# Bonus sums of an RWKV-7 layer as two accumulating single-pass products of a split operand

## The chip, the cores and the metric

The kernel runs on one core of a Trainium2 chip. A core has TensorE (PE: matmuls, with its weight loads shown as PEld), VectorE (DVE), ScalarE (ACT), GpSimd (POOL) and SyncE (SP, which here only issues DMAs). The engines run beside each other, each taking its own instructions in order, and wait for one another through semaphores. The metric is the device time of one execution in microseconds (us), given as the median of several runs. Times inside the kernel come from one profiled execution, counted from the start of its span.

## The reference

It is one step of a two-layer decoder for a prompt of 272 positions (16 learned meta tokens and 256 others) and 8 samples of one position each: 280 columns in all. Layer A is RWKV-7 time mixing with 64 heads of 64 channels (width 4096), layer B sliding-window attention. What matters here are the last lines of layer A, after the recurrence has given `y`:

```python
y = (y - mean) * lax.rsqrt(var + GN_EPS) * gn_g + gn_b
y = y + jnp.sum(r_h * k_h * r_k, axis=-1, keepdims=True) * v_h
y = y.reshape(B, T, WIDTH).astype(dt) * jax.nn.silu(z)
```

For each position and head, `r * k * r_k` is summed over the head's 64 channels; the sum scales that head's `v`. This term is called the bonus here. All inputs and outputs are float32.

## The kernel before

Activations lie with channels on the 128 partitions and positions along the free dimension, so one tile of 128 rows holds two heads, and the sum over a head's channels runs across partitions.

Weight products are done in three single-pass products each. Both operands are split into a part `hi`, cast to the type float32r on ACT, and a remainder `lo = x - hi`, computed on DVE (`split`, L192: the cast is L195, the subtraction L197). `mm3` (L216) accumulates hi*hi, hi*lo and lo*hi in one PSUM bank (L218, L219, L220). A plain float32 operand goes to TensorE as it is, in one matmul call.

Layer A's weights come in units of 256 input rows by 256 outputs: a DMA into `raw`, the cast `whi`, the subtraction `wlo`, each with five buffers (L199). `products` (L708) walks over them one after another, in pieces of six matmuls: r, k, v and z for each block of channels, and lastly part of the output projection. Layer A proper (`phase_a`, L577) starts after the first blocks of k and v, at about 130 us, and its last pieces run at about 1280 us.

Into this row of weight products, other work is woven by `drive` (L609). It runs generators beside `products`: `preps` (per pair of channel blocks, 16 preparations `prep(u)`, each for four heads), `main` (the chunked recurrence), `decodes` (the samples) and epilogues. Each `yield n` means that the generator goes on n pieces later; `self.pp_free` asks in addition that the single spare PSUM bank was last taken at least three pieces ago. TensorE's instructions keep exactly this written order (`pe_order`). On ACT, DVE, POOL and SP, a planner orders the instructions by a simulated timeline, by readiness and priority; some instructions are told not to go ahead of a given weight subtraction (`issue_after`). Each engine's order is fixed when the kernel is built.

`prep(u)` (L857) does, in this order: load the second matrices of the two low-rank products (`lraw`, L868), split them into `lhi` and `llo` (L871 to L873, one buffer each), four low-rank products `ps_l` by `mm3` (L880), then load k, r, the key norms and v, and form decay, `kk`, `a` and the changed `k` on ACT and DVE; a transpose for the samples (`ps_sm`, L934); and lastly the bonus:

- L944, DVE: `rk = r * r_k * k`, 128x272, once for each of the two channel blocks, into a tile with two buffers (tag "sq", shared with `km`, L900)
- L950, PE: `ps_bo`, the product of `rk` with the constant `crbo`, a 128x128 matrix that holds a 64x64 block of ones for each of the two heads. This sums over each head's channels and puts the sum in all of its 64 rows
- L951, DVE: `v` is multiplied by the sum; L952, ACT: the group norm's bias is added

The first of the two sums is written into PE's order five pieces after `rk` (three in the first two preparations), the second four pieces later. The next odd-numbered preparation begins right behind, with its load; its split is written three pieces later and its first low-rank product four pieces after that. An even-numbered preparation also waits for the step `prep_e` of the one before.

`crbo` is loaded once in phase 0 (L274, L275), by a DMA on SP's queue.

Of the kernel before, what the change touches and what calls it, by code (L numbers as in the profile page):

```python
# [12 lines left out]
F32 = mybir.dt.float32  # L13
F32R = mybir.dt.float32r
# [11 lines left out]
L = NM + SEQ  # L26
# [7 lines left out]
LR = 96  # L34
# [14 lines left out]
C_BO, C_SEL = 368, 496  # L49
# [60 lines left out]
class Kernel:  # L110
# [155 lines left out]
    def params(self):  # L266
        nc, I = self.nc, self.I
        dma = nc.sync.dma_start
        dma(self.ct, I['consts'][:, :C_TOTA])
        dma(self.par, I['consts'][:, C_PAR:])  # L270
        yield

        self.cr = {}
        self.cr[C_BO] = self.cp.tile([128, 128], F32, name="crbo")  # L274
        dma(self.cr[C_BO], I['consts'][:, C_BO:C_BO + 128])  # L275

        self.sel = self.cp.tile([128, 32], F32, name="selt")
        nc.gpsimd.memset(self.sel, 0.0)
        dma(self.sel[:, 0:2], I['consts'][:, C_SEL:C_SEL + 2])
        self.half = self.cp.tile([128, 2], F32, name="half")  # L280
        for i in range(2):
            nc.vector.memset(self.half[:, i:i + 1], 0.5 - i)

        self.par2 = self.cp.tile([128, 128], F32, name="par2")
        ts = nc.gpsimd.tensor_scalar
        ts(self.par2[:, 0:64], self.par[:, P_W0:P_W0 + 64], 0.5, None, op0=ALU.mult)
        ts(self.par2[:, 64:96], self.par[:, P_KA:P_KA + 32], 0.5, None, op0=ALU.mult)
        ts(self.par2[:, 96:128], self.par[:, P_KA:P_KA + 32], -0.5, 1.0, op0=ALU.mult, op1=ALU.add)
# [19 lines left out]
    def phase0(self):  # L308
# [11 lines left out]
        for a, b in ((0, 4), (4, 8), (8, 12), (12, 14), (14, 16)):  # L320
            dma(xz[:, a:b], I['xT'][:, a:b])
        params = self.params()
        next(params)

        sq = dx = ph.tile([128, KT, N], F32, name="dx")
# [531 lines left out]
    def prep(self, u):  # L857
        nc, rp, I = self.nc, self.rp, self.I
# [3 lines left out]
        dma = nc.sync.dma_start  # L862
# [5 lines left out]
        dma(raw, I['lw2'][u])  # L868
        if u:
            yield 3  # L870
        hi = rp.tile([LR, 512], F32R, tag="lhi", name=f"lhi_{u}")  # L871
        lo = rp.tile([LR, 512], F32R, tag="llo", name=f"llo_{u}")
        self.split(hi, lo, raw)  # L873
        ws = [(hi[:, 256 * i:256 * i + 256], lo[:, 256 * i:256 * i + 256]) for i in range(2)]
        wa = [w("cl"), w("ta")]
        for i, (hi, lo) in enumerate(ws):
            for j in range(2):
                yield 3 if i or j else 4 if u else 14, self.pp_free
                ps = self.pp_bank(f"ps_l{i}{j}_{u}")
# [53 lines left out]
        ps = self.pp_bank(f"ps_sm{u}")  # L933
# [8 lines left out]
        def rk_of(j):  # L942
            rk = rp.tile([128, L], F32, tag="sq", bufs=2, name=f"rk{j}_{u}")
            V.scalar_tensor_tensor(rk, rT[:, j, :L], self.pcol(P_RK, p0 + j), kT[:, j, :L], op0=MU, op1=MU)  # L944
            return rk
        rk = [rk_of(j) for j in range(2)]
        for j in range(2):
            yield 5 - j if u > 1 else 3, self.pp_free
            ps = self.pp_bank(f"ps_bo{j}_{u}")
            nc.tensor.matmul(ps[:, :L], self.cr[C_BO], rk[j], start=True, stop=True)  # L950
            tt(vT[:, j, :L], ps[:, :L], vT[:, j, :L], op=MU)  # L951
            A.activation(vT[:, j, :L], vT[:, j, :L], AF.Identity, bias=self.pcol(P_GB, p0 + j))  # L952
        self.U[u] = dict(PC=self.PC, bonus=vT, kT=kT, rT=rT, kk=kk, a=a, cl=cl)
# [1015 lines left out]
```

## Time and profile before

| | |
|---|---|
| time, median of 3 runs | 2121.87 us (2119.55 to 2125.27) |
| profiled execution, time | 2132.89 us |
| its span | 2131.1 us, mean granted TensorE clock 0.989 |
| busy: PE, DVE, ACT | 2073.1 (97%), 1685.4 (79%), 1252.9 us (59%) |
| bonus products `ps_bo` | 64 records on PE, 21.2 us busy, from 176.4 to 1116.8 us |
| bonus scaling L951 on DVE | 32 records, 419 to 442 ns each |
| `rk` L944 on DVE | 32 records, 486 to 502 ns each |

A line of the profile names the source line (L950), the engine, the operation, the tile written and the tiles read (`ps_bo<-rk,crbo`), its shape and how many instructions it groups. "128*128 128x272" on PE means a stationary operand of 128x128 and a moving one of 128x272. In the order of time, a row begins with start and duration in us; where several like instructions follow each other they are merged (x2). A bracket such as [0.93 <-PE ps_r L219] is the idle time of the engine before that instruction, and what ended it. Matmuls overlap in the pipeline, so their durations are longer than the distance from one to the next. One plain float32 matmul call of L950 shows as two records on PE.

### The profile page before, as it was taken

The page shows a single profiled execution, that of the slowest core. Times are in us where ns is not written, and L with a number is a line of the kernel's source. Part 1 is how long each engine was busy: PE and PEld are TensorE (multiplying, and loading weights), DVE is VectorE, ACT ScalarE, POOL GpSimd, SP SyncE. Part 2 cuts the span into 40 slices and gives each one's busy share as a digit, 9 for nine tenths or more (in the row PEclk, how much of TensorE's full clock was granted, in tenths as well). Part 3 has the DMA queues.
Part 4 walks back from the last instruction along what each step waited for, and adds up shares of the span by engine and source line. Part 5 has one row for each costly group of instructions (what it writes and reads, how often), then busy time and mean ns, then how long its engine had stood idle before and what let it go on. Part 6 is the DMA issues. An engine that isn't in the chain of part 4 may idle for free.

```text
span 2131.1 us, 55813 instructions
## 1 busy us (share of the span) xinstructions
PE 2073.1 (97%) x21420; PEld 1971.4 (93%) x21420; DVE 1685.4 (79%) x4080; ACT 1252.9 (59%) x2757; POOL 121.5 (6%) x188
## 2 busy tenths in 40 slices
PE   9999999899999989999999999999999999999997
PEld 7999898899899989999999999999999999999997
DVE  7866767687678768888888787987888888878885
ACT  3456666576765757767675455565565655644443
POOL 0011100001010010100100001100000000000000
PEclk9999999999999999999999999999999999999999
DMA  7997667668657766777656678757455454567774
GB/s 256 315 314 243 177 215 241 183 186 289 208 178 211 251 207 204 214 225 212 203 161 222 217 239 253 237 186 223 143 149 171 137 158 135 178 203 252 227 220 134
DMA packets 276356, 446.28 MB, mean 209 GB/s; under 512 B 54056, under 2 KB 97768, under 8 KB 275696
## 3 DMA queue, kind: packets, MB, share of 16 engines
q1 hardware_dynamic: 275656, 441.66, 66.4%
q8 instruction: 168, 2.75, 0.5%
q10 hardware_dynamic: 432, 1.05, 0.1%
q14 instruction: 100, 0.82, 0.1%
HBM read 381.69 MB, written 65.03 MB: 210 GB/s over the span
## 4 chain that ended last, share of the span: by engine, by line
PE 60%; DVE 3%; DMA 2%; issue 1%; ACT 1%; POOL 0%; POOLq 0%; DVEq 0%; SPq 0%; ACTq 0%
PE ps_z L218 6%; PE ps_z L219 5%; PE ps_z L220 5%; PE ps_ob L218 3%; PE ps_ob L220 3%; PE ps_ob L219 3%; PE ps_q L218 3%; PE ps_q L220 3%; PE ps_q L219 3%; PE ps_oa L219 2%; PE ps_oa L218 2%; PE ps_oa L220 2%; PE ps_o L218 1%; PE ps_o L219 1%; PE ps_o L220 1%
## 5 line engine op out<-in xcount | busy, mean ns | idle before, releaser
L218 PE MATMUL ps_z<-mhlm,whi_z 128*128 128x280 f32 x512 | 158.7, 310 | 0.4 <-ACT st L789 0.4
L220 PE MATMUL ps_z<-mhlm,wlo_z 128*128 128x280 f32 x512 | 149.6, 292 | 2.7 <-issue 2.7
L218 PE MATMUL ps_q<-bmh,whi_qb 128*128 128x264 f32 x512 | 150.0, 293 | 0.4 <-ACT whi_qb L195 0.3
L219 PE MATMUL ps_z<-mhlm,whi_z 128*128 128x280 f32 x512 | 149.8, 292 | 0.0
L218 PE MATMUL ps_z<-bmh,whi_zb 128*128 128x264 f32 x512 | 147.5, 288 | 0.0
L220 PE MATMUL ps_q<-bmh,wlo_qb 128*128 128x264 f32 x512 | 145.6, 284 | 0.6 <-DVE wlo_qb L197 0.6
L219 PE MATMUL ps_q<-bml,whi_qb 128*128 128x264 f32 x512 | 145.6, 284 | 0.0
L219 PE MATMUL ps_z<-bml,whi_zb 128*128 128x264 f32 x512 | 145.4, 284 | 0.0
L220 PE MATMUL ps_z<-bmh,wlo_zb 128*128 128x264 f32 x512 | 145.4, 284 | 0.0
L218 PE MATMUL ps_ob<-ghi,whi_ob 128*128 128x264 f32 x512 | 145.3, 285 | 0.0
L220 PE MATMUL ps_ob<-ghi,wlo_ob 128*128 128x264 f32 x512 | 144.6, 284 | 0.0
L219 PE MATMUL ps_ob<-glo,whi_ob 128*128 128x264 f32 x512 | 144.6, 283 | 0.0
L195 ACT CAST whi_ob<-raw_ob 128x512 fp32r<-128x512 f32 x128 | 79.1, 620 | 96.9 <-PE ps_ob L219 75.4
L195 ACT CAST whi_oa<-raw_oa 128x512 fp32r<-128x512 f32 x128 | 79.2, 620 | 89.7 <-PE ps_oa L219 27.9
L197 DVE TENSOR_TENSOR wlo_r<-raw_r,whi_r 128x512 fp32r<-128x512 f32 x128 | 87.5, 688 | 48.7 <-ACT whi_r L195 46.3
L218 PE MATMUL ps_v<-mhlm,whi_v 128*128 128x280 f32 x384 | 121.4, 316 | 0.4 <-ACT st L789 0.4
L218 PE MATMUL ps_k<-mhlm,whi_k 128*128 128x280 f32 x384 | 120.4, 313 | 1.1 <-ACT st L789 1.1
L197 DVE TENSOR_TENSOR wlo_v<-raw_v,whi_v 128x512 fp32r<-128x512 f32 x128 | 87.4, 687 | 41.0 <-ACT whi_v L195 37.8
L195 ACT CAST whi_v<-raw_v 128x512 fp32r<-128x512 f32 x128 | 79.1, 618 | 66.5 <-PE ps_v L219 39.5
L195 ACT CAST whi_zb<-raw_zb 128x512 fp32r<-128x512 f32 x128 | 78.2, 619 | 62.6 <-PE ps_z L219 39.3
L220 PE MATMUL ps_k<-mhlm,wlo_k 128*128 128x280 f32 x384 | 112.9, 294 | 1.2 <-issue 1.1
L219 PE MATMUL ps_k<-mhlm,whi_k 128*128 128x280 f32 x384 | 113.0, 294 | 0.0
(473 smaller groups left out, 7584.2 us busy)
## 6 DMA issues: line engine op xcount, KB each, us to landing
raw_k<-a_w_rkvz SPq DMA_DIRECT2D x128, 256.0 KB
raw_v<-a_w_rkvz SPq DMA_DIRECT2D x128, 256.0 KB
raw_r<-a_w_rkvz SPq DMA_DIRECT2D x128, 256.0 KB
raw_z<-a_w_rkvz SPq DMA_DIRECT2D x128, 256.0 KB
raw_oa<-a_w_out SPq DMA_DIRECT2D x128, 256.0 KB
raw_qb<-b_w_qz SPq DMA_DIRECT2D x128, 256.0 KB
raw_zb<-b_w_qz SPq DMA_DIRECT2D x128, 256.0 KB
raw_ob<-b_w_o SPq DMA_DIRECT2D x128, 256.0 KB
```

The lines of the kernel that those rows point to most:

```text
L195: self.nc.scalar.copy(hi, src)
L197: return self.nc.vector.tensor_tensor(lo, src, hi.bitcast(F32), op=ALU.subtract)
L218: mm(ps, wh, xh, start=start, stop=False)
L219: mm(ps, wh, xl, start=False, stop=False)
L220: return mm(ps, wl, xh, start=False, stop=stop)
```

## The change

Only layer A's bonus sums change. The block matrix of ones is loaded in phase 0 into a scratch tile and cast on ACT into a float32r tile `ones`. `rk` is split like the weights: a cast on ACT and a subtraction on DVE for each channel block. The sum is then two accumulating single-pass products, hi and lo of `rk`, both with `ones`. Ones are exact in float32r, so no third product is needed.

The two halves of `rk`, for both channel blocks, lie in the buffers of the low-rank matrices (tags "lhi" and "llo"), which are made larger for it: 128x544 where they were 96x512. The places in TensorE's order, the `yield`s, are the same.

```diff
-        self.cr = {}
-        self.cr[C_BO] = self.cp.tile([128, 128], F32, name="crbo")
-        dma(self.cr[C_BO], I['consts'][:, C_BO:C_BO + 128])
+        self.ones = self.cp.tile([128, 128], F32R, name="ones")
+        ones = self.ph.tile([128, 128], F32, name="blocks")
+        dma(ones, I['consts'][:, C_BO:C_BO + 128])
+        nc.scalar.copy(self.ones, ones)
...
-        hi = rp.tile([LR, 512], F32R, tag="lhi", name=f"lhi_{u}")
-        lo = rp.tile([LR, 512], F32R, tag="llo", name=f"llo_{u}")
+        hi = rp.tile([128, 544], F32R, tag="lhi", name=f"lhi_{u}")[:LR, :512]
+        lo = rp.tile([128, 544], F32R, tag="llo", name=f"llo_{u}")[:LR, :512]
         self.split(hi, lo, raw)
...
             rk = rp.tile([128, L], F32, tag="sq", bufs=2, name=f"rk{j}_{u}")
             V.scalar_tensor_tensor(rk, rT[:, j, :L], self.pcol(P_RK, p0 + j), kT[:, j, :L], op0=MU, op1=MU)
-            return rk
-        rk = [rk_of(j) for j in range(2)]
+            self.split(two[0][:, j], two[1][:, j], rk)
+        two = [rp.tile([128, 2, L], F32R, tag=n, name=f"rk{n}{u}") for n in ("lhi", "llo")]
+        for j in range(2):
+            rk_of(j)
         for j in range(2):
             yield 5 - j if u > 1 else 3, self.pp_free
             ps = self.pp_bank(f"ps_bo{j}_{u}")
-            nc.tensor.matmul(ps[:, :L], self.cr[C_BO], rk[j], start=True, stop=True)
+            for i in range(2):
+                nc.tensor.matmul(ps[:, :L], self.ones, two[i][:, j], start=i == 0, stop=i == 1)
             tt(vT[:, j, :L], ps[:, :L], vT[:, j, :L], op=MU)
```

## The prediction

> **What bounds the kernel now.** I read the profile's page first, then the busy times by stage over the part where the changed code runs, then the waits of TensorE there, and last the instructions in order of time around some of the bonus sums.
>
> The page, first line and busy times:
>
> ```profile
> span 2131.1 us, 55813 instructions
> PE 2073.1 (97%) x21420; PEld 1971.4 (93%) x21420; DVE 1685.4 (79%) x4080; ACT 1252.9 (59%) x2757; POOL 121.5 (6%) x188
> ```
>
> The stages of layer A in which bonus sums run (columns: stretch, its length, busy us and instructions of PE, PEld, DVE, ACT, POOL, granted clock, DMA share, GB/s):
>
> ```profile
> 130.00:300.00 170.00, 162.57 (x1704) 156.87 (x1703) 110.91 (x232) 112.31 (x245) 18.62 (x35) 0.97 0.74 227
> 300.00:500.00 200.00, 190.86 (x2348) 177.26 (x2347) 150.42 (x346) 126.96 (x293) 11.62 (x21) 0.98 0.68 212
> 500.00:700.00 200.00, 195.41 (x2614) 182.59 (x2613) 147.14 (x331) 131.99 (x289) 19.57 (x29) 0.98 0.67 207
> 700.00:900.00 200.00, 192.59 (x2333) 178.03 (x2332) 154.13 (x355) 135.07 (x306) 17.46 (x26) 0.98 0.73 228
> 900.00:1100.00 200.00, 193.18 (x2593) 181.84 (x2593) 175.58 (x407) 139.99 (x310) 15.04 (x27) 0.99 0.66 199
> 1100.00:1280.00 180.00, 175.39 (x2176) 165.98 (x2177) 145.52 (x323) 97.72 (x199) 4.61 (x7) 1.00 0.70 221
> ```
>
> PE is busy for 1110.0 of these 1150 us, DVE for 883.7 (77%), with its highest share, 88%, from 900 to 1100. So PE sets the pace, with 40 us of holes, and DVE is the next engine. What PE waits for between 130 and 1280 us, the five longest sums:
>
> ```profile
> PE ps_yt L1271 <- DVE vT L1272: 11.0, 6, 7.3
> PE ps_so L1098 <- DVE TN L1077: 5.5, 2, 4.3
> PE ps_so L1104 <- issue: 3.3, 1, 3.3
> PE ps_sm L934 <- POOL sm L931: 3.2, 1, 3.2
> PE ps_ch L1201 <- ACT W L1192: 2.9, 3, 2.2
> ```
>
> The first two and the last, 19.4 us, are late work of DVE and ACT. The bonus sum itself is not among them. Its matmuls, and one of them in PE's order of time:
>
> ```profile
> L950 PE MATMUL ps_bo<-rk,crbo x64: 390/392/661, 176.4 to 1116.8; 128*128 128x272 f32 x64
> ```
> ```profile
> 409.71 0.29 PE L220 MATMUL ps_v<-mhlm,wlo_v 128*128 128x280 f32 x1
> 409.84 0.62 PE L950 MATMUL ps_bo<-rk,crbo 128*128 128x272 f32 x2
> 410.10 0.49 PE L218 MATMUL ps_v<-mhlm,whi_v 128*128 128x280 f32 x1
> 410.43 0.29 PE L219 MATMUL ps_v<-mhlm,whi_v 128*128 128x280 f32 x1
> ```
>
> The durations overlap, so I count from end to end. L220 ends at 409.71 + 0.29 = 410.00, the pair of records that is one plain float32 product at 410.46, the next L218 at 410.59, L219 at 410.72. The bonus product holds PE for **0.46 us**; a single-pass product of 280 columns for 0.13. Nothing waits around it: before and after it PE runs without a hole.
>
> **The change part by part.**
>
> *PE.* 64 records are 32 products of 0.46 us: 14.7 us go. In their place come 64 single-pass products of 272 columns. That form isn't in the trace; its price is bounded by the 280-column products above (0.13) and the 264-column ones of layer B:
>
> ```profile
> 1459.05 0.28 PE L220 MATMUL ps_q<-bmh,wlo_qb 128*128 128x264 f32 x1
> 1459.18 0.28 PE L218 MATMUL ps_q<-bmh,whi_qb 128*128 128x264 f32 x1
> 1459.30 0.28 PE L219 MATMUL ps_q<-bml,whi_qb 128*128 128x264 f32 x1
> ```
>
> These follow each other in 0.12 to 0.13. I take 0.125, midway: 64 x 0.125 = 8.0 us come. PE saves 14.7 - 8.0 = **6.7 us** (7.0 at 0.12, 6.4 at 0.13). The number of PE records stays 2 per sum, so weight loads and sequencer work don't grow.
>
> The Trainium skill, "TensorE: Matmul & The Clock Gate", section "Back-to-back issue gap", gives N/2.4 + 2.5 ns for a single-pass product, 116 ns for 272 columns; by it, as an estimate, 7.4 us would come and 7.3 go. The trace disagrees by about 10 ns: the rule gives 119 ns for 280 columns, where the rows above show 130.
>
> *ACT and DVE.* The split adds 32 casts on ACT and 32 subtractions on DVE, each of 128x272. Near rows, the first from ACT's order of time, then DVE groups between 160 and 1120 us:
>
> ```profile
> 18.03 0.66 ACT L195 CAST mhld<-mst 128x560 fp32r<-128x560 f32 x1 [3.34 <-DVE mst L390]
> 18.59 1.65 ACT L195 CAST whi_k<-raw_k 128x512 fp32r<-128x512 f32 x3
> ```
> ```profile
> L197 DVE TENSOR_TENSOR wlo_r<-raw_r,whi_r 128x512 fp32r<-128x512 f32 x115 | 78.5, 688 | 37.6 <-ACT whi_r L195 35.3 <-DMA vt<-N 1.2 <-DMA raw_r<-a_w_rkvz 0.8
> ...
> L944 DVE SCALAR_TENSOR_TENSOR rk<-rT,par,kT 128x272 f32<-128x272 f32 x32 | 14.8, 495 | 3.2 <-DMA rT<-rd 3.2
> ```
>
> A cast of 512 elements holds ACT for 1.65/3 = 0.55, so one of 272 for between 0.29 (in proportion) and 0.55; I take 0.35 for the fixed part: 11 us. A subtraction lies between 0.37 (688 x 272/512) and 0.49; at 0.43 it is 14 us. Neither engine is the bound: DVE has 1150 - 883.7 = 266 us idle there, ACT 506. The cover is that idle time. Without it each split costs up to its 0.35 + 0.43 plus two hand-overs, about 1 us. What leaks through: DVE's load rises by 14/884 = 1.6%, and 1.6% of the 19.4 us of waits on DVE and ACT is 0.3; for queueing, which grows faster than load, I take **0.5 us** (0 to 3; a better planned order, which would be a gain, stands with the rivals).
>
> *Latency ahead of the sum.* The product used to need only rk; now it needs rk, a cast on ACT and a subtraction on DVE. The narrowest of the 16 places has rk on DVE at 200.43 and its sum on PE at 206.93:
>
> ```profile
> 200.43 0.50 DVE L944 SCALAR_TENSOR_TENSOR rk<-rT,par,kT 128x272 f32<-128x272 f32 x1
> ```
> ```profile
> 206.93 0.62 PE L950 MATMUL ps_bo<-rk,crbo 128*128 128x272 f32 x2
> ```
>
> That is 6.0 us of slack. The chain needs 0.35 + 0.43 and, in either queue, at worst a pair of 512-element items ahead (1.1 and 1.4): 3.3 us. Cost 0. If the slack were gone, PE would stall in order, with the weight products behind it.
>
> *The shared buffers.* rk's halves take the buffers of the low-rank weights (lhi, llo), one each. So the next preparation's lhi and llo may be written only when the second bonus sum of this one is done. Before, the cast ran long ahead. First pair of preparations, on ACT, DVE and PE:
>
> ```profile
> 162.46 0.62 ACT L195 CAST lhi<-lraw 96x512 fp32r<-96x512 f32 x1
> ...
> 179.32 0.62 ACT L195 CAST whi_r<-raw_r 128x512 fp32r<-128x512 f32 x1 [0.93 <-PE ps_r L219]
> ```
> ```profile
> 176.70 0.68 DVE L197 TENSOR_TENSOR llo<-lraw,lhi 96x512 fp32r<-96x512 f32 x1
> ```
> ```profile
> 179.20 0.62 PE L950 MATMUL ps_bo<-rk,crbo 128*128 128x272 f32 x2
> ...
> 185.05 0.29 PE L218 MATMUL ps_l<-lt4h,lhi 96*128 96x280 f32 x1
> ```
>
> The sum ends at 179.82, the first reader starts 5.2 us later; read the same way, this first pair is the narrowest of the 15. The new chain is a cast (0.62) and a subtraction (0.68) with up to 1.1 and 1.4 queued ahead: 3.8 us. It fits. Queued behind the waiting lhi on ACT are weight casts; but ACT already waits for PE there, as the row at 179.32 shows, so it has time to lose. Cost 0, bounded by 5.2 - 3.8 = 1.4 us of margin.
>
> *Start-up.* The block of ones is loaded into a scratch tile and cast once on ACT, some 0.3 us, at a time when ACT is idle for microseconds at a stretch (3.34 before the row at 18.03); its first reader is at 176.4. Cost 0.
>
> *What stalls swallow.* Saved time is kept only if the next stall's cause moves with PE. The longest stall:
>
> ```profile
> 380.35 0.93 DVE L897 SCALAR_TENSOR_TENSOR kk<-kT,par,kk 128x280 f32<-128x280 f32 x2 [4.76 <-DMA kk<-kr]
> ```
> ```profile
> 386.56 0.90 PE L1271 MATMUL ps_yt<-consts,Y 128*128 128x128 f32 x3 [7.30 <-DVE vT L1272]
> ```
>
> DVE stood there on a DMA of key norms. Eight sums lie before it (4 preparations): 8 x 0.21 = 1.7 us saved. The norms come out of earlier PE products, so part of the stall moves along; I take **0.8 us** lost, half (0 to 1.7).
>
> *Sum.* -6.7 + 0.5 + 0.8 = **-5.4 us**. On the profiled execution's own 2132.9 us (span 2131.1, 1.8 around it) that gives 2127.5. That execution lies 11.0 above the median of the runs; the saving carries over to them: 2121.9 - 5.4 = **2116.5 us**.
>
> **The rivals.** About 0.3% (6.4 us) is what a measurement of this kernel can tell from no change, and the full PE saving is just that size.
>
> *Swallowed.* PE's time goes into the next waits, and the end hardly moves. For it: 19.4 us of PE's waits end on DVE or ACT, which get more work. Against: in the long runs between stalls ACT and DVE wait for PE (the row at 179.32; the 35.3 us of DVE behind ACT's casts follow from the same). If a quarter of 6.7 passes and the 0.5 is added, 2121.9 - 1.7 + 0.5 = 2121.
>
> *The low-rank buffers bind* (the other side). If DVE or ACT brings llo more than 5.2 us after the sum, PE stalls at its first reader. What such a stall costs is to be seen where PE waited 1.23 us:
>
> ```profile
> 672.79 1.20 PE L1125 MATMUL ps_so<-TT,ET 32*32 32x32 f32 x64 [1.23 <-ACT ET L1120]
> ```
> ```profile
> 671.50:674.20 2.70, 1.47 (x67) 1.37 (x67) 2.67 (x6) 1.72 (x3) 0.39 (x1) 1.00 0.89 262
> 674.20:677.70 3.50, 3.50 (x15) 3.27 (x15) 1.51 (x3) 0.99 (x2) 0.28 (x1) 0.51 0.97 263
> ```
>
> After it the granted clock is 0.51 for 3.5 us, which loses 1.7 more: 1.2 + 1.7 = 2.9 us a stall. From three stalls on it eats the saving; at 4 it gives 2121.9 - 5.4 + 11.6 = 2128. The same page of the Trainium skill (section "Why this matters for your kernels") asks only that idle gaps stay under about 3 us; by that a stall of 1.2 us would cost 1.2, four would cost 4.8 and the result be 2121. The trace disagrees: the clock halved after 1.23 us.
>
> *A better order.* ACT and DVE are ordered anew by the planner, and stalls that are accidents of the order can go. One long wait on DVE with its half-clock stretch (4.3 + 1.7 in the second wait above) less gives 2116.5 - 6.0 = 2110.5.
>
> *It doesn't do what it says*: the new products run as slowly as the old one. Then 64 x 0.46 = 29.4 come for 14.7: 2137. Against it: every weight product of this form runs at 0.13.
>
> **How the numbers follow.** Forecast 0.45, own range 2113 to 2120; a third of it lies beyond 0.3%. Swallowed 0.18 (2119 to 2124). Buffers bind, or DVE's load leaks on the same scale, 0.16. Better order 0.20. Not as said 0.01. Faster by over 0.3%: 0.15 of the forecast and 0.19 of the better order, 0.34. Within: 0.30 of the forecast, 0.17 swallowed, 0.01 each of buffers and order, 0.49. Slower: 0.15 of the buffers, 0.01 each of swallowed and not as said, 0.17. The range of 8 in 10 reaches from 2109 (a better order) to 2128 (four stalls).
>
> **What would show it.** Two records of 272 columns per sum, ending 0.12 to 0.13 apart, and PE's time on the sums down from 14.7 to 8.0. lhi's casts right behind the second sum, on ACT, and no wait of ps_l longer than 1 us. The sums no later behind rk than PE's order puts them. Waits of PE on DVE in 130 to 1280 us near 19 us as before. I am wrong if a wait at ps_l or ps_bo shows, if PE's waits on DVE grow by over 3 us, or if the sums take over 0.3 us each.

## The result

| | before | changed |
|---|---|---|
| time, median of 20 runs each | 2124.31 us (2119.55 to 2128.32) | 2118.46 us (2114.5 to 2124.2) |
| ratio to before | | 0.9978, 95% interval 0.9970 to 0.9987 |
| profiled execution, time and span | 2132.89, 2131.1 us | 2118.32, 2116.5 us |
| PE, DVE, ACT busy | 2073.1, 1685.4, 1252.9 us | 2064.9, 1697.8, 1263.8 us |

The change saves 0.22% or, with 2124 us for the whole, 4.7 us (2.8 to 6.4); the two medians themselves differ by 5.9 us. 5.4 us were forecast (2116.5 us, range 2109 to 2128), within the 0.3% called "no change to be told" there. One execution of the products-only kernel below took 5016 us and is in no ratio.

The two profiled executions lie 14.6 us apart, two and a half times the difference of the medians: the one of before is 8.6 us above the median of its 20 runs, the one of the change is at its own. So no sum can be read off the two profiles; single places can. The page of the changed kernel, first line and busy times:

```profile
span 2116.5 us, 55871 instructions
PE 2064.9 (98%) x21420; PEld 1965.8 (93%) x21420; DVE 1697.8 (80%) x4112; ACT 1263.8 (60%) x2790; POOL 122.5 (6%) x188
```

One bonus sum in PE's order of time (start, duration):

```profile
405.52 0.29 PE L220 MATMUL ps_v<-mhlm,wlo_v 128*128 128x280 f32 x1
405.65 0.29 PE L954 MATMUL ps_bo<-rklhi,ones 128*128 128x272 f32 x1
405.78 0.29 PE L954 MATMUL ps_bo<-rkllo,ones 128*128 128x272 f32 x1
405.90 0.29 PE L218 MATMUL ps_v<-mhlm,whi_v 128*128 128x280 f32 x1
```

The ends are 405.81, 405.94, 406.07, 406.19: a product holds PE for 0.13 and 0.13, as the weight products around it do. The split on ACT and DVE (groups between 160 and 1120 us):

```profile
L195 ACT CAST rklhi<-rk 128x272 fp32r<-128x272 f32 x32 | 12.7, 418 | 11.4 <-DVE rk L945 11.4
```
```profile
L197 DVE TENSOR_TENSOR rkllo<-rk,rklhi 128x272 fp32r<-128x272 f32 x32 | 13.1, 434 | 0.5 <-ACT rklhi L195 0.4
```

The shared buffers, at the first pair of preparations, on PE, ACT and DVE:

```profile
177.45 0.29 PE L954 MATMUL ps_bo<-rkllo,ones 128*128 128x272 f32 x1
...
182.97 0.29 PE L218 MATMUL ps_l<-lt4h,lhi 96*128 96x280 f32 x1
```
```profile
178.14 0.62 ACT L195 CAST lhi<-lraw 96x512 fp32r<-96x512 f32 x1
```
```profile
178.88 0.68 DVE L197 TENSOR_TENSOR llo<-lraw,lhi 96x512 fp32r<-96x512 f32 x1
```

lhi, which ran 17 us ahead of the second sum before, now starts 0.4 us behind its end (177.74), and llo is done 3.4 us before the first low-rank product. What PE waits for between 130 and 1280 us (total, times, longest):

```profile
PE ps_yt L1275 <- DVE vT L1276: 8.0, 2, 6.9
PE ps_so L1102 <- DVE TN L1081: 6.1, 2, 3.5
...
PE ps_bo L954 <- ACT vk L854: 2.0, 1, 2.0
...
PE ps_bo L954 <- DVE vT L955: 1.5, 2, 1.3
```

The third row, also a wait for the spare bank (ACT copies a transpose out of it), stood in the kernel before with 1.6 us. The last row is new. No sum waits there for its halves: the second sum of the first preparation waits for DVE to scale the first one and so free the only spare bank.

```profile
177.22 0.39 PE L954 MATMUL ps_bo<-rklhi,ones 128*128 128x272 f32 x1 [1.27 <-DVE vT L955]
```
```profile
170.78 0.46 DVE L197 TENSOR_TENSOR rkllo<-rk,rklhi 128x272 fp32r<-128x272 f32 x1
...
171.76 0.43 DVE L197 TENSOR_TENSOR rkllo<-rk,rklhi 128x272 fp32r<-128x272 f32 x1
...
176.74 0.43 DVE L955 TENSOR_TENSOR vT<-ps_bo,vT 128x272 f32<-128x272 f32 x1
```

Yet the split has a part in it. DVE is busy without a gap from 168.33 to this scaling, and the two subtractions lie in that queue, with 0.38 and 0.36 us to the next start: 0.74 of the 1.27 us. In the second profile of the change (e5 below) this wait doesn't appear.

And the second row shows where the split's work on DVE gets onto the path. DVE's order of time ahead of one of its two waits, PE's wait, and the stage's busy times (columns as in the prediction; the last but two is the granted clock):

```profile
908.28 0.20 DVE L1075 TENSOR_TENSOR stmp<-NL 128x52 f32<-128x52 f32 x1
...
909.09 0.68 DVE L197 TENSOR_TENSOR wlo_z<-raw_z,whi_z 128x512 fp32r<-128x512 f32 x1
909.70 0.43 DVE L197 TENSOR_TENSOR rkllo<-rk,rklhi 128x272 fp32r<-128x272 f32 x1
910.05 0.20 DVE L1077 TENSOR_TENSOR NL<-NL,stmp 128x52 f32<-128x52 f32 x1
910.17 0.43 DVE L197 TENSOR_TENSOR rkllo<-rk,rklhi 128x272 fp32r<-128x272 f32 x1
910.52 0.68 DVE L197 TENSOR_TENSOR wlo_z<-raw_z,whi_z 128x512 fp32r<-128x512 f32 x1
911.12 0.18 DVE L1075 TENSOR_TENSOR stmp<-NL 128x28 f32<-128x28 f32 x1
911.42 0.69 DVE L197 TENSOR_TENSOR wlo_z<-raw_z,whi_z 128x512 fp32r<-128x512 f32 x1
912.03 0.18 DVE L1077 TENSOR_TENSOR NL<-NL,stmp 128x28 f32<-128x28 f32 x1
912.25 1.04 DVE L1081 STREAM_TRANSPOSE TN<-NL 128x512 f32<-128x512 f32 x1
```
```profile
913.43 1.27 PE L1102 MATMUL ps_so<-TN,Noff 32*32 32x16 f32 x81 [2.56 <-DVE TN L1081]
```
```profile
910.80:913.40 2.60, 0.07 (x1) 0.00 (x1) 2.44 (x6) 0.59 (x1) 0.46 (x1) 0.89 1.02 323
913.50:919.60 6.10, 6.10 (x146) 6.03 (x147) 1.26 (x3) 3.96 (x6) 0.20 (x1) 0.50 0.85 278
```

L1075 to L1081 is a chain of small DVE steps (the triangular substitution of the recurrence), and PE needs its end. DVE takes its instructions in order with hardly a gap here, and each of the two subtractions, 0.43 long, stands between two steps of that chain. PE waits 2.56 us and then runs 6.1 us at half clock, which is another 3.05 lost. The same place before, on DVE and PE, with the stage behind it:

```profile
919.47 0.20 DVE L1071 TENSOR_TENSOR stmp<-NL 128x52 f32<-128x52 f32 x1
...
920.88 0.20 DVE L1073 TENSOR_TENSOR NL<-NL,stmp 128x52 f32<-128x52 f32 x1
921.15 0.69 DVE L197 TENSOR_TENSOR wlo_z<-raw_z,whi_z 128x512 fp32r<-128x512 f32 x1
921.76 0.18 DVE L1071 TENSOR_TENSOR stmp<-NL 128x28 f32<-128x28 f32 x1
921.97 0.19 DVE L1073 TENSOR_TENSOR NL<-NL,stmp 128x28 f32<-128x28 f32 x1
922.20 1.03 DVE L1077 STREAM_TRANSPOSE TN<-NL 128x512 f32<-128x512 f32 x1
```
```profile
923.38 1.26 PE L1098 MATMUL ps_so<-TN,Noff 32*32 32x16 f32 x128 [1.24 <-DVE TN L1077]
```
```profile
923.50:929.50 6.00, 6.00 (x283) 5.74 (x279) 3.04 (x7) 4.50 (x7) 0.20 (x1) 1.00 0.86 235
```

There PE waited 1.24 us and the clock stayed whole. From the step at 919.47 to the transpose the chain took 2.73 us; now, from 908.28, it takes 3.97. Of these 1.24 more, the two subtractions make 0.70 (to the next starts); nearly all the rest is a weight subtraction (911.42) that the order before had behind the chain. The longer wait for TN has become shorter (4.3 to 3.5), so that the sum is 6.1 where it was 5.5.

In the runs below, the wait at this place is 1.24 to 1.26 us with no subtraction of rk on DVE (the plain product twice, the products alone in both layouts, one product, the subtraction on GpSimd), 2.56 or 2.57 with one split on DVE (the split alone, the change again, the unread split) and 2.86 with two. Out of line are the buffers alone, 2.34 with no split, and the two kernels with later sums, 4.09 and, without a split, 2.79. The clock behind it varies: in the second profile of the change the half-clock stretch is 3.4 us, half as long as here.

### The profile page after: what moved, and what is told of

It reads as the page before. It is cut to its first block, busy times and chain, and to the rows that moved or that the text cites. A ratio compares the mean times of both kernels' runs of the same rounds, so it can differ in the third digit from the quotient of the medians.

```text
span 2116.5 us, 55871 instructions
## 1 busy us (share of the span) xinstructions
PE 2064.9 (98%) x21420; PEld 1965.8 (93%) x21420; DVE 1697.8 (80%) x4112; ACT 1263.8 (60%) x2790; POOL 122.5 (6%) x188
## 4 chain that ended last, share of the span: by engine, by line
PE 87%; DVE 5%; ACT 3%; DMA 3%; issue 2%; SPq 0%; POOL 0%; DVEq 0%; POOLq 0%; ACTq 0%
PE ps_z L218 6%; PE ps_z L219 6%; PE ps_z L220 6%; PE ps_k L218 3%; PE ps_ob L218 3%; PE ps_ob L220 3%; PE ps_v L218 3%; PE ps_ob L219 3%; PE ps_r L218 3%; PE ps_q L218 3%; PE ps_q L220 3%; PE ps_q L219 3%; PE ps_k L219 3%; PE ps_k L220 3%; PE ps_v L220 3%; PE ps_v L219 3%
## 5 line engine op out<-in xcount | busy, mean ns | idle before, releaser
L218 PE MATMUL ps_v<-mhlm,whi_v 128*128 128x280 f32 x384 | 119.8, 312 | 0.4 <-ACT st L790 0.4
L218 PE MATMUL ps_k<-mhlm,whi_k 128*128 128x280 f32 x384 | 119.1, 310 | 1.0 <-ACT st L790 1.0
L219 PE MATMUL ps_v<-mhlm,whi_v 128*128 128x280 f32 x384 | 112.7, 293 | 0.0
```

What stands on the lines that cost most here:

```text
L218: mm(ps, wh, xh, start=start, stop=False)
L219: mm(ps, wh, xl, start=False, stop=False)
```

## The experiments

Each ratio is to the kernel before, run beside it on the same chip; us are (ratio - 1) x 2124. TensorE's part in the edits: one plain product 0.458 us, one single-pass product 0.125.

**The parts alone.** First the split without the new products. rk is split into the low-rank buffers (enlarged as in the change, not shown below), nobody reads the halves, the plain product stays:

```diff
+            self.split(two[0][:, j], two[1][:, j], rk)
             return rk
+        two = [rp.tile([128, 2, L], F32R, tag=n, name=f"rk{n}{u}") for n in ("lhi", "llo")]
         rk = [rk_of(j) for j in range(2)]
```

> The kernel before, with rk split into hi and lo as in the change (32 casts on ACT, 32 subtractions on DVE, written into the low-rank buffers), but the sum still the plain float32 product of rk; nobody reads the two halves. TensorE's work is that of before. Prediction's theory: the split leaks 0.5 us (0 to 3): ratio to before 1.0002, at most 1.0014. Rival, the engines' load costs as much as half the saving: +3 us or more, ratio 1.0015 or above.

Measured: 1.0003 (0.9994 to 1.0012), +0.6 us (-1.3 to +2.5). As forecast; the rival's +3 lies outside.

The products without the split:

```diff
-            rk = rp.tile([128, L], F32, tag="sq", bufs=2, name=f"rk{j}_{u}")
-            V.scalar_tensor_tensor(rk, rT[:, j, :L], ...)
-            self.split(two[0][:, j], two[1][:, j], rk)
+            V.scalar_tensor_tensor(two[:, j], rT[:, j, :L], ...)
-        two = [rp.tile(...) for n in ("lhi", "llo")]
+        two = rp.tile([128, 2, L], F32R, tag="lhi", name=f"rkhi{u}")
...
-                nc.tensor.matmul(ps[:, :L], self.ones, two[i][:, j], ...)
+                nc.tensor.matmul(ps[:, :L], self.ones, two[:, j], ...)
```

> The changed kernel without the split: DVE writes rk rounded to float32r at once, and both single-pass products read this same tile, so the bonus comes out doubled and rounded. No cast, no subtraction; the tile lies in the buffer of lhi alone. TensorE's work is that of the change. Prediction's theory: -6.7 saved, 0.8 swallowed: -5.9 us, ratio 0.9972. Rival, the split's load leaks 3 us: -8.4 or more here, ratio 0.9960. Rival, stalls swallow the saving: as the change or less, -5 to -2 us.

Measured, over four executions: 0.9954 (0.9941 to 0.9967), -9.8 us (-12.5 to -7.0): more than TensorE's own saving of 6.7. The -5.9 of the prediction's theory lies outside the interval; the number is the one that a leak of 3 us gave. A second layout below tests this.

The shared buffers alone (the low-rank buffers enlarged as in the change, not shown below):

```diff
-            rk = rp.tile([128, L], F32, tag="sq", bufs=2, name=f"rk{j}_{u}")
+            rk = rp.tile([128, 544], F32R, tag=("lhi", "llo")[j], name=f"rk{j}_{u}").bitcast(F32)[:, :L]
```

> The kernel before, with rk of the two channel blocks written into the buffers of lhi and llo (float32 values, as before), so that the next preparation's lhi and llo wait for the bonus sums; no split, the plain float32 product. Prediction's theory: the wait is covered, 0 us, ratio 1.0000 within 0.0007. Rival, the low-rank buffers bind: stalls at the first low-rank product of 1.2 us and more with half clock behind, +3 us each, ratio 1.0015 or above and a wait row for ps_l.

Measured: 0.9996 (0.9987 to 1.0005), -0.8 us (-2.8 to +1.1). The low-rank buffers don't bind. Buffers of their own for rk's halves would take 4.25 kB per partition, and the opposite, the change without sharing, wasn't tried.

The parts don't add up: split and products together would give -9.2 us, and the change gave -4.7. The next runs ask where the rest went.

**How much of TensorE's time reaches the end.** The plain product issued twice:

```diff
-            nc.tensor.matmul(ps[:, :L], self.cr[C_BO], rk[j], start=True, stop=True)
+            for _ in range(2):
+                nc.tensor.matmul(ps[:, :L], self.cr[C_BO], rk[j], start=True, stop=True)
```

> The kernel before with each float32 bonus product issued twice, the second overwriting the first: 32 x 0.46 = 14.7 us more on TensorE, nothing else. Prediction's theory: of the 3.7 us ahead of the long stall half goes into it, the rest passes: +12.9 us, ratio 1.0061. Rival, time on TensorE here goes into or out of the waits: a quarter passes, +3.7 us, ratio 1.0017.

Measured: 1.0047 (1.0033 to 1.0062), +10.0 us (+7.0 to +13.2) for 14.7 us of work. The sums of that run are 128 records on PE, of the same length as before:

```profile
L951 PE MATMUL ps_bo<-rk,crbo x128: 390/392/661, 176.4 to 1119.7; 128*128 128x272 f32 x128
```

0.68 of it passes (0.48 to 0.90). The rival of a quarter is out; the 12.9 of the theory is inside the interval, at its upper side.

**One product instead of two.** The products-only kernel with a single product:

```diff
-            for i in range(2):
-                nc.tensor.matmul(ps[:, :L], self.ones, two[:, j], start=i == 0, stop=i == 1)
+            nc.tensor.matmul(ps[:, :L], self.ones, two[:, j], start=True, stop=True)
```

The change ran once more beside it:

> The changed kernel once more, beside the next three. The split alone cost 0.6 us and the products alone saved 9.8, but the change saved 4.6: either chance (the change comes out at -7 to -9 here, ratio about 0.996), or the split costs some 5 us once the sums read it (ratio 0.9978 again).

Measured for the change again: 0.9984 (0.9970 to 0.9997), -3.4 us (-6.4 to -0.6), in line with the 20 runs.

> rk rounded to float32r by DVE as it writes it, and a single product of it: no cast, no subtraction, the remainder lo left out of the sum. TensorE does 32 x (0.458 - 0.125) = 10.7 us less than before. If 70% of TensorE's time passes on to the end, as in the run with the product twice: -7.3 us, ratio 0.9966. If all of it passes and the split was what held the change back: -10.7 to -14 us, ratio 0.9950 to 0.9934.

Measured: 0.9957 (0.9941 to 0.9972), -9.1 us (-12.5 to -5.9) for 10.7 us less on TensorE: 0.85 passes (0.55 to 1.17), between the two expectations and with both in the interval. Its median is 2113.70 us, that of the change beside it 2121.36. Against the products alone in this layout (-9.8), the 4.0 us that TensorE does less show no gain (+0.7, -3.6 to +5.0 with the intervals combined).

**Does the split cost by its load, or because sums wait for it?** The change with its split, but the products read rk itself:

```diff
-            rk = rp.tile([128, L], F32, tag="sq", ...)
+            rk = rp.tile([128, L], F32R, tag="sq", ...)
-            self.split(two[0][:, j], two[1][:, j], rk)
+            self.split(two[0][:, j], two[1][:, j], rk.bitcast(F32))
+            return rk
...
-                nc.tensor.matmul(ps[:, :L], self.ones, two[i][:, j], ...)
+                nc.tensor.matmul(ps[:, :L], self.ones, rk[j], ...)
```

> The change with its split on ACT and DVE (hi, lo written into the low-rank buffers as in the change), but both single-pass products read rk itself, rounded by DVE as it writes it, so the sums don't wait for the split and the bonus comes out doubled. TensorE's work is that of the change. If the split costs by its load on DVE and ACT: as the change, -4.6 us, ratio 0.9978. If it costs because the sums wait behind cast and subtraction: as the products alone, -9.8 us, ratio 0.9954.

Measured: 0.9997 (0.9981 to 1.0013), -0.6 us (-4.0 to +2.8). The -9.8 of the second expectation is out, and the change itself, where the halves are read, is no slower. By load it should have come out like the change: the -4.6 of the 20 runs lies just outside the interval, the -3.4 of the change beside it inside. What a split costs that nobody reads, the next runs show.

The same kernel without the split, and with two of them (the line of `split` taken out, or written twice; without it the low-rank buffers, too, are those of before):

> The products alone in another layout: both single-pass products read rk as DVE rounds it, in rk's own two buffers as before, and the low-rank buffers are those of before (the bonus comes out doubled). It is the kernel with the unread split, less the split, and less the shared buffers. If the split's load is what costs: -9.8 again, ratio 0.9954, and some 5 us or more under the unread split. If the first such run was helped by its order: -5 to -7, ratio 0.9977 to 0.9967.

> The kernel with the unread split, with cast and subtraction done twice each: 64 casts on ACT and 64 subtractions on DVE for the same products of TensorE (the bonus comes out doubled). If a split costs 5 us by load: another 5 on top of the unread split, ratio about 1.002. By the prediction's 0.5 us a split: as the unread split within 1 us, ratio 0.9995 to 1.0002.

Measured: without 0.9979 (0.9966 to 0.9993), -4.5 us (-7.2 to -1.5); twice 1.0017 (1.0003 to 1.0032), +3.6 us (+0.6 to +6.8). So none, one and two splits give -4.5, -0.6 and +3.6 us, some 4 us each (8.1 for two, 3.9 to 12.3 with the intervals combined). The prediction's 0.5 a split is outside the interval of the last. The two longest waits of PE on DVE in the three kernels, none, one and two splits (130 to 1290 us):

```profile
PE ps_yt L1273 <- DVE vT L1274: 8.5, 4, 6.6
PE ps_so L1100 <- DVE TN L1079: 5.8, 2, 4.6
```
```profile
PE ps_yt L1275 <- DVE vT L1276: 7.3, 3, 6.5
PE ps_so L1102 <- DVE TN L1081: 7.0, 2, 4.5
```
```profile
PE ps_yt L1276 <- DVE vT L1277: 10.3, 4, 8.0
PE ps_so L1103 <- DVE TN L1082: 8.0, 2, 5.1
```

The wait for TN, the end of the chain that the subtractions stood in above, grows from 5.8 to 7.0 and 8.0; both together from 14.3 to 14.3 and 18.3, and all waits of PE on DVE there from 17.1 to 19.4 and 22.2.

The products alone came to -4.5 in this layout and -9.8 in the other, with the same work on every engine. The two differ in the buffers that hold rk and, as each kernel is planned anew, in the order of ACT, DVE and SP; which of them makes the 5 us wasn't shown.

**The subtraction on GpSimd:**

```diff
-            self.split(two[0][:, j], two[1][:, j], rk)
+            A.copy(two[0][:, j], rk)
+            G.tensor_tensor(two[1][:, j], rk, two[0][:, j].bitcast(F32), op=SU)
```

> The change with rk's remainder lo subtracted on GpSimd, which is busy for 6% of the span, in place of DVE: DVE has the 14 us of subtractions less, ACT the same casts. If the split costs by its load on DVE: toward the products alone, -7 to -10 us, ratio 0.9967 to 0.9954. If the load costs little: as the change, -3 to -5 us, ratio 0.9985 to 0.9978. A subtraction on GpSimd should take over 1 us, so sums that come late behind it would show as waits of ps_bo.

Measured: 1.0004 (0.9990 to 1.0017), +0.8 us (-2.1 to +3.6), so the gain of the change is gone. The subtraction there:

```profile
L947 POOL TENSOR_TENSOR rkllo<-rk,rklhi x32: 751/922/1352, 168.0 to 1088.5; 128x272 fp32r<-128x272 f32 x32
```

It takes 0.75 to 1.35 us, and no sum waits for it in the trace. Why freeing DVE of 13 us doesn't show is open: neither "DVE's load alone" nor "the load costs little" gives this number. The trace shows where time came back, not why. Between 130 and 1290 us PE waits 41.1 us in all, where it waited 33.3 in the change, though the wait for TN shown above is back at 1.26. DVE is busy for 902.5 us there, only 8.4 less than in the change, as its weight subtractions take longer (`wlo_r` 710 ns in the mean, 691 in the change).

**Later sums**, and later with one product:

```diff
-            yield 5 - j if u > 1 else 3, self.pp_free
+            yield 7 - j if u > 1 else 5, self.pp_free
```

> The change with the first sum of each preparation written two pieces later into TensorE's order (seven instead of five, five instead of three; the second sum seven minus one, or five): 1.5 us more slack behind the split. If sums wait for the split or for the spare bank: faster than the change by 2 us or more, ratio 0.9968 or below. If the prediction's slack was wide enough: the same as the change, ratio 0.9978 within 0.0008.

> One product of rk as DVE rounds it (lo left out of the sum), with the sums written two pieces later as in the run with later sums. If both gains add: -9.1 - 2 = -11 us, ratio 0.9948. If the later place only moves stalls about: as the one product, ratio 0.9957.

Measured: the change with later sums 0.9972 (0.9957 to 0.9988), -5.9 us (-9.1 to -2.5); one product, later 0.9955 (0.9940 to 0.9970), -9.6 us (-12.7 to -6.4). The first lies between its two expectations and can't be told from the change; the second is the one product's -9.1 again. The later place is worth nothing that these runs show. The one product beats both kernels by some 5 us and more, at the price of rk's remainder.

## Why the prediction was right

The twelve ratios other than that with GpSimd fit, roughly, a sum of two terms: 0.84 of what TensorE's work changes, plus 2.4 us per split (least squares over them, weighted by their intervals). The kernels scatter about it by more than their intervals: some 2 us, and over 4 for the products alone (-4.2) and the doubled split (+4.5). That I put to the planned orders, but it was not shown. By the prediction's steps:

- *PE, -6.7.* Right: the sums' records end 0.125 apart in the median, so 64 x 0.125 = 8.0 us stand where 14.7 did. TensorE's 0.125 is the middle of the bounds that the 264- and 280-column rows gave. The rule of the Trainium skill that the prediction names beside it ("TensorE: Matmul & The Clock Gate", section "Back-to-back issue gap") is given there for an isolated product, which the prediction does not say; by it a sum's product would take 0.116, as an estimate.
- *ACT and DVE, 11 and 14 us.* 12.7 and 13.1 busy. Right.
- *What leaks through, 0.5 (0 to 3).* Probably too small, but inside its own range. The split alone under the old product gives 0.6, the runs with none, one and two splits some 4 us each, the fit 2.4 (1.2 without the doubled split). The step scaled PE's waits by DVE's mean load. But DVE works in order, and some of its chains end in a wait of PE: two subtractions of 0.43 in such a chain delay it by nearly their full length, and PE's stall was followed by half clock. The idle time of DVE elsewhere in the stage doesn't help at that place. This is shown at that place; that it makes the whole of the leak is not. PE's waits on DVE, which were to stay near 19 us, come to 16.7 in the change (19.0 before, and 19.0 in the second profile of the change).
- *What stalls swallow, 0.8 of 6.7.* 0.88 was to pass; the runs give 0.68 and 0.85 for more and less work, the fit 0.84: 1.1 swallowed. Right in size.
- *Latency ahead of the sum, 0.* Right: no sum waits for its halves. The prediction named a wait of ps_bo as a sign against itself, and one of 1.27 us shows, but for the spare bank, which it had not counted. As a sign it was badly chosen: the kernel before has a wait of ps_bo, too, of 1.6 us.
- *The shared buffers, 0.* Right: lhi directly behind the sum, llo 3.4 us ahead of its readers, and 0.9996 for the buffers alone. The rival built on them is out.
- *Start-up, 0.* Right: at 165 us both kernels stand at the same matmul within 0.1 us.

By the two terms the change should have saved 0.84 x 6.7 - 2.4 = 3.2; 4.7 and 3.4 were measured. So the gain of TensorE and the share that passes were right by their mechanism, but that -5.4 came within 1 us of the first number is in part luck: by the fit the leak is 2 us short, and the kernels scatter by as much.

## What to carry to other kernels

Where TensorE is at 97%, count its time from end to end of its products; here some 0.8 of a saving reached the end. Work put onto an engine with a quarter of its time idle need not be free if that engine carries serial chains in order that TensorE waits for: look where the new instructions fall in its queue, not at its mean load. One profiled execution may lie 9 us off the median, so price single places from it and take sums from many runs.

## What was not expected of the hardware

How long a hole of TensorE lowers its clock. The stall before the first bonus sums, in the kernel before and in the changed one, on PE, and the same stretch behind it in each (before first; the granted clock is the last but two):

```profile
172.41 0.42 PE L934 MATMUL ps_sm<-consts,sm 128*96 128x128 f32 x1 [3.17 <-POOL sm L931]
```
```profile
170.37 0.31 PE L935 MATMUL ps_sm<-consts,sm 128*96 128x128 f32 x1 [1.22 <-POOL sm L932]
```
```profile
172.50:175.90 3.40, 3.40 (x16) 3.40 (x16) 2.65 (x7) 1.45 (x3) 0.20 (x1) 0.50 1.01 329
```
```profile
172.50:175.90 3.40, 3.40 (x27) 3.23 (x26) 3.40 (x10) 1.70 (x3) 0.00 (x0) 1.00 0.90 248
```

3.17 us halve the clock for 3.4 us; 1.22 here do not. In the changed kernel a hole of 2.03 leaves it at 1.00, too:

```profile
862.17 0.39 PE L954 MATMUL ps_bo<-rklhi,ones 128*128 128x272 f32 x1 [2.03 <-ACT vk L854]
```
```profile
862.20:866.00 3.80, 3.80 (x29) 3.80 (x30) 3.37 (x7) 3.62 (x7) 0.00 (x0) 1.00 0.74 225
```

but after the hole of 1.23 in the prediction it halved. So a hole of one to two us may or may not cost a half-clock stretch, and the prediction's 2.9 us for each was the dear end. The Trainium skill, "TensorE: Matmul & The Clock Gate", section "What's actually happening", says that the activity is judged in windows of 3.4 us that run freely, and that half clock follows at least one idle window. The half-clock stretches, 3.4 us and, from 912.84 to 919.67, 6.8, agree with such a length; the holes of 1.23 and 2.56 us do not agree with the demand for a whole idle window. Whether it matters how a hole lies to the windows, no run here shows.

GpSimd's subtraction of 128x272 was in most places cheaper than the "over 1 us" that I expected: 0.92 us in the median, from 0.75 to 1.35.
